# Modulation vectors beside the second branch projection: the sample's half from VectorE to ScalarE and GpSimd

## The chip, the cores and the metric

The kernel runs on one core of a Trainium2 chip. The core has five engines that work side by side, each through its own instructions in order: TensorE (PE in the profile; PEld is its weight load), VectorE (DVE), ScalarE (ACT), GpSimd (POOL) and SyncE (SP), which here only issues DMAs. The metric is the device time of one execution in microseconds (us), lower is better.

## The reference, cut to what matters

One layer of a streaming encoder is computed for two groups of rows at once, a prompt of 512 frames and a sample of 64. The change touches the modulation vectors alone, and it runs while the second branch is projected:

```
mod = silu(c) @ w_ada + b_ada                  # c: one vector for the prompt, one for the sample
sh1, sc1, gt1, sh2, sc2, gt2 = split(mod, 6)   # w_ada is 1024 x 6144
...
mixed = (g_attn * (o_attn @ w_branch_attn) + g_ssm * (y @ w_branch_ssm)) @ w_out
x = x + gt1 * mixed
h2 = rms_normalize(x) * g_norm_ffn * (1.0 + sc2) + sh2
```

## The kernel before, in words

Every matrix product splits its operands into a high and a low part (`wh`, `wl` of the weights, `yh`, `yl` of the rows), and TensorE multiplies high by high, low by high and high by low. The 576 columns of prompt and sample together go through in two halves of 288. For the second branch projection (the loop over `a` in range(8) that makes `ps = fm(f"pbs{a}", ...)`), each output tile a takes 16 row tiles k, so 96 matmuls. Its weights come in two chunks of eight k: a DMA fills `raw`, ScalarE writes `wh`, VectorE writes `wl` as `raw - wh`. Three buffers of each exist, so ScalarE can write the next `wh` once TensorE has left an old one. When a tile a is done, VectorE makes `g` from the PSUM result, adds it to `m`, and `m` is split into `mh` (ScalarE) and `ml` (VectorE) for the output projection.

Beside this, `ada_columns(u, adv)` (L792, called at L1604 to L1606) computes five sets of 512 modulation columns, u = 5 to 9, without TensorE's main work: `w_ada` comes in row blocks of 128 (tile `adr`), and for each row block kt and each group s (0 the prompt, 1 the sample) one VectorE instruction multiplies the block by the group's column of `sil` and adds it to the accumulator `aacc` of that group. After eight blocks `ada_sum` (L809) adds over the partitions: eight matmuls against the constant `pick` (four for each group, `px<-aacc,pick` in the order, sixteen records in the profile), VectorE copies the result (`ra`), TensorE transposes it (`py<-ident,ra`), VectorE adds the bias (`modc`). These results are wanted in the stages behind.

The order is not that of the code. `Plan.add` (L289) records each instruction, `Plan.order` plays a schedule with a table of costs and writes every engine's list in that order, and each engine then follows its list. The plan treats GpSimd instructions that read wide operands, and VectorE instructions with two wide SBUF inputs, as exclusive to each other (`op.port`). A TensorE instruction is placed at least `slack` after its inputs in the plan: 3.0 us for the `pick` matmuls, 0.25 us (`SLACK`) otherwise, the transposition of `ra` included. All instructions go through one line (L544), so the profile tells them apart by their tiles.

Of the kernel before, what the change touches and what calls it, by code (L numbers as in the profile page):

```python
# [5 lines left out]
F32 = mybir.dt.float32  # L6
F32R = mybir.dt.float32r
BF = mybir.dt.bfloat16
AF = mybir.ActivationFunctionType
OP = mybir.AluOpType  # L10
# [3 lines left out]
P = 128  # L14
# [216 lines left out]
def _cols(v):  # L231
    n = 1
    for k in v.shape[1:]:
        n *= k
    return n


def is_psum(v):
    return isinstance(v, View) and v.base.kind == "psum"
# [9 lines left out]
class Plan:  # L249
# [39 lines left out]
    def add(self, eng, fn, args, kw):  # L289
        op = Op()  # L290
        op.eng, op.fn, op.args, op.kw = eng, fn, args, kw
        op.i, op.succ, op.pools, op.bytes, op.mm = len(self.ops), [], set(), 0, False
        op.prio = op.i - self.offset
        outs = [args[0] if args else kw["out"]]
        if kw.get("accum_out") is not None:
            outs.append(kw["accum_out"])
        outs = [o for o in outs if isinstance(o, View)]
        ins = [a for a in list(args[1:]) + [v for k, v in kw.items() if k not in ("out", "accum_out")] if isinstance(a, View)]
        deps = {}
        for v in ins:  # L300
            self._touch(op, v, False, deps)
        for v in outs:
            self._touch(op, v, True, deps)
        for o in self.also:
            deps.setdefault(o.i, "raw")
        op.deps = deps
        op.slack = self.slack if eng == "tensor" else 0.0
        wide = sum(1 for v in ins if not is_psum(v) and _cols(v) > 1)
        op.port = eng == "gpsimd" and wide > 0 and fn != "dma_start" or eng == "vector" and wide > 1
        op.dur, op.dur_dma = self.cost(op, outs, ins)  # L310
        self.ops.append(op)
        return op
# [239 lines left out]
def build(tc, I, O):  # L552
    R = Plan(tc)
    vec, act, pool, pe, sync = R.vec, R.act, R.pool, R.pe, R.sync
# [11 lines left out]
    def px(name, tag="px"):  # L566
        return psum.tile([P, 512], F32, name=name, tag=tag, bufs=2)
# [49 lines left out]
    raws, outs, outs_made = {}, {}, []  # L617
# [107 lines left out]
    sil = adp.tile([P, 8, 32], F32, name="sil")  # L725
# [63 lines left out]

    acc_last = {}  # L790

    def ada_columns(u, pl, nacc=1, bufs=2, nk=2, tags=None, late=False):  # L792

        acc = [pl.tile([P, 512], F32, name=f"aacc{u}{s}", tag=tags[s] if tags else f"aacc{s}", bufs=nacc) for s in range(2)]
        for k0 in range(0, 8, nk):
            raw = pl.tile([P, nk, 512], F32, name=f"wada{u}_{k0}", tag=tags[2 + k0 // nk % 2] if tags else "adr", bufs=bufs)
            (pool if u == 10 else sync).dma_start(raw, w_ada[P * k0:P * (k0 + nk), 512 * u:512 * u + 512].rearrange("(k p) n -> p k n", p=P))
            for j in range(nk):
                kt = k0 + j
                for s in range(2):  # L800
                    if kt == 0:
                        vec.tensor_scalar(acc[s], raw[:, j], sil[:, kt, s:s + 1], None, op0=OP.mult)
                    else:
                        acc_last[u, s] = vec.scalar_tensor_tensor(acc[s], raw[:, j], sil[:, kt, s:s + 1], acc[s], op0=OP.mult, op1=OP.add)
        if late:
            return acc
        ada_sum(u, acc, px(f"padc{u}"))

    def ada_sum(u, acc, p, p2=None):  # L809
        with R.prio(4000):  # L810
            R.slack = 3.0
            with R.after([acc_last[u, s] for s in range(2)]):
                for s in range(2):
                    for g in range(4):
                        pe.matmul(p[32 * g:32 * g + 32, 0:P], pick[:, s], acc[s][:, P * g:P * g + P], start=(s == 0), stop=(s == 1),
                                  tile_position=(0, 32 * g))
            R.slack = SLACK
            ada_out(u, p, p2)
# [26 lines left out]
    for tb in range(5):  # L845
# [5 lines left out]
        for k4 in range(2):  # L851
            p = px(f"pxn{tb}_{k4}")
            for j in range(4):
                kt = 4 * k4 + j
# [53 lines left out]
    with R.prio(-1500):  # L908
        for tb in range(5):
# [9 lines left out]
            for k4 in range(2):  # L919
                o, i = st[:, 4 * k4:4 * k4 + 4, :n], p[:, k4].rearrange("p (k q) -> p k q", k=4)[:, :, :n]  # L920
# [166 lines left out]
    with R.prio(0):  # L1087
        ada_columns(4, adx, 1, 1, 1)
# [88 lines left out]
    for c in range(5):  # L1177
        o, i0 = (p[0][:32, P * c:P * c + P], P) if c < 4 else (p[1][:32, :NS], NS)
# [21 lines left out]
    for b in (4, 1, 2, 3):  # L1200
# [4 lines left out]
        s = ix.tile([P, n], F32, name=f"score{b}")  # L1205
# [106 lines left out]
    for kv in range(NKV):  # L1312
# [21 lines left out]
        for un in units + [None]:  # L1334
            nxt = None
            if un is not None:
                b, qs, k0, n, nk, v0, w = un
# [244 lines left out]
    for s, dst in ((0, O["conv_prompt"]), (1, O["conv_sample"])):  # L1582
        p = px(f"pcvo{s}")
        pe.transpose(p[:96, :P], cvo[:, s].rearrange("p j a -> p (j a)"), ident)
        o = sd.tile([96, P], F32, name=f"cvoT{s}")
# [14 lines left out]
    with R.prio(0):  # L1600
        for u in range(4 + NADX, 4 + NADX + NADA):
            ada_columns(u, gtp, 2)
    adv = R.mkpool("adav", reuse_waits="tile")
    with R.prio(-2000):  # L1604
        for u in range(4 + NADX + NADA, 10):
            ada_columns(u, adv)  # L1606
    yh_p = R.mkpool("yhl", reuse_waits="tile")
    yh = [yh_p.tile([P, T], F32R, name=f"yh{k}") for k in range(16)]
    yl = [yh_p.tile([P, T], F32R, name=f"yl{k}") for k in range(16)]
# [368 lines left out]
    xo, acc = {}, {}  # L1978
# [184 lines left out]
    for o in order:  # L2163
# [27 lines left out]
        else:  # L2191
            s, r, p = o[1:]
# [72 lines left out]
```

## Time and profile before

| | |
|---|---|
| median of 3 runs | 1355.69 us (1355.35 to 1356.16) |
| span of the profiled execution, first to last instruction | 1353.9 us |
| TensorE (PE) busy | 1341.1 us, 99% |
| VectorE (DVE) busy | 1138.9 us, 84% |
| ScalarE (ACT) busy | 756.7 us, 56% |
| GpSimd (POOL) busy | 247.9 us, 18% |
| TensorE's granted clock, mean | 0.999 of full speed |

The page states the span of the profiled execution and no other time for it; the median of the runs lies 1.8 us above that span, which is what the execution takes around its first and last instruction. Busy time is the time in which an engine had an instruction running. Times of rows are counted from the first instruction.

### The profile page before, as it was taken

Reading aid. Unit: us, or ns where it says so; the run is one execution under the profiler, and the core shown is the slowest. Engines: PE = TensorE matmul, PEld = TensorE weight load, DVE = VectorE, ACT = ScalarE, POOL = GpSimd, SP = SyncE. Lnnn points to the kernel's source line nnn. Section 1 sums busy time; section 2 is a strip of 40 time slices with the busy share of each in tenths; the row PEclk is TensorE's granted clock in tenths of the full one; section 3 lists DMA queues with packets and bytes.
Section 4 is the critical chain, followed back from the end, with each engine's and each line's share of the span. In section 5 each row is a group of like instructions: output and inputs, shape, how many; then the busy total and the mean of one; then the engine's idle time right before and its main releaser. Section 6 shows DMA issues by size and latency. Waiting matters only on the chain.

```text
span 1353.9 us, 27909 instructions
## 1 busy us (share of the span) xinstructions
PE 1341.1 (99%) x10677; PEld 1307.3 (97%) x10677; DVE 1138.9 (84%) x2303; ACT 756.7 (56%) x1597; POOL 247.9 (18%) x381
## 2 busy tenths in 40 slices
PE   8999999999999999999999999999999999999998
PEld 6999999999999999999999999999999999999998
DVE  5788999887777788888887688867799999878997
ACT  5445343787777666666565342225576666665453
POOL 2312011230301234545463300002100000000000
PEclk9999999999999999999999999999999999999999
DMA  9762435574754464454445688747533343324352
GB/s 300 228 182 82 112 107 155 126 184 108 170 139 119 139 177 112 116 151 129 133 122 172 216 290 256 232 139 250 153 94 94 99 129 102 94 78 138 98 163 64
DMA packets 268454, 201.35 MB, mean 149 GB/s; under 512 B 25553, under 2 KB 239681, under 8 KB 268321
## 3 DMA queue, kind: packets, MB, share of 16 engines
q1 hardware_dynamic: 263056, 183.40, 46.2%
q0 software_dynamic: 4976, 16.05, 5.9%
q8 instruction: 83, 1.36, 0.4%
q14 instruction: 51, 0.41, 0.1%
q10 hardware_dynamic: 288, 0.13, 0.0%
HBM read 157.75 MB, written 28.96 MB: 138 GB/s over the span
## 4 chain that ended last, share of the span: by engine, by line
PE 93%; DVE 4%; issue 1%; ACT 1%; DMA 0%; POOL 0%; DVEq 0%; POOLq 0%; ACTq 0%
PE mm L544 64%; PE py L544 17%; PE px L544 12%; DVE score L544 1%; DVE m L544 1%; DVE wl L544 0%; DMA B<-in_w_down 0%; DVE tok L544 0%; DVE xs L544 0%; DVE rr L544 0%; ACT wh L544 0%; ACT wl L544 0%; POOL tok L544 0%; DVE xn L544 0%; DVE kst L544 0%
## 5 line engine op out<-in xcount | busy, mean ns | idle before, releaser
L544 ACT ACTIVATE wh<-raw 128x1024 fp32r<-128x1024 f32 (+3 forms) x144 | 140.5, 979 | 170.5 <-PE mm L544 133.0
L544 PE MATMUL mm<-hTl,wh 128*128 128x288 f32 (+1 forms) x1024 | 232.7, 302 | 0.9 <-DVE hTl L544 0.9
L544 PE MATMUL mm<-hTh,wh 128*128 128x288 f32 (+1 forms) x1024 | 231.6, 303 | 0.6 <-ACT wh L544 0.5
L544 PE MATMUL mm<-hTh,wl 128*128 128x288 f32 (+1 forms) x1024 | 230.3, 302 | 0.0
L544 PEld LDWEIGHTS mm<-hTl,wh 128*128 128x128 f32 (+1 forms) x1024 | 166.9, 189 | 3.7 <-DVE hTl L544 1.4
L544 PEld LDWEIGHTS mm<-hTh,wh 128*128 128x128 f32 (+1 forms) x1024 | 166.0, 189 | 4.0 <-ACT hTh L544 1.0
L544 PEld LDWEIGHTS mm<-hTh,wl 128*128 128x128 f32 (+1 forms) x1024 | 165.8, 189 | 1.8 <-issue 0.7
L544 DVE TENSOR_TENSOR wl<-raw,wh 128x1024 fp32r<-128x1024 f32 (+2 forms) x99 | 120.9, 1223 | 25.5 <-ACT wh L544 24.3
L544 POOL DMA_DIRECT2D wl<-raw x24 | 22.1, 919 | 472.2 <-PE px L544 313.8
L544 DVE SCALAR_TENSOR_TENSOR cu<-xc,wc,cu 128x579 f32<-128x579 f32 x96 | 83.8, 873 | 2.0 <-ACT cu L544 1.0
L544 PE MATMUL mm<-wh,hTl 128*128 128x256 f32 x256 | 73.2, 286 | 0.0
L544 PE MATMUL mm<-wl,hTh 128*128 128x256 f32 x256 | 72.5, 284 | 0.0
L544 PE MATMUL mm<-wh,hTh 128*128 128x256 f32 x256 | 72.4, 285 | 0.0
L544 DVE SCALAR_TENSOR_TENSOR aacc<-adr,sil,aacc 128x512 f32<-128x512 f32 x84 | 59.1, 753 | 5.0 <-DMA adr<-in_w_ada 4.7
L544 PE MATMUL mm<-yh,wl 128*128 128x288 f32 x256 | 55.2, 296 | 0.0
L544 PE MATMUL mm<-yh,wh 128*128 128x288 f32 x256 | 55.0, 296 | 0.0
L544 PE MATMUL mm<-yl,wh 128*128 128x288 f32 x256 | 54.9, 296 | 0.0
L544 PE MATMUL mm<-xhS,wh 128*128 128x290 f32 (+1 forms) x248 | 54.8, 296 | 0.0
L544 ACT ACTIVATE P<-lg,mn 128x128 f32<-128x128 f32 (+4 forms) x72 | 41.7, 580 | 23.1 <-DVE mn L544 22.0
L544 PE MATMUL mm<-xhS,wl 128*128 128x290 f32 (+1 forms) x232 | 51.2, 296 | 0.0
L544 ACT ACTIVATE dec<-dec,nacs 128x128 f32<-128x128 f32 x128 | 42.4, 392 | 14.4 <-POOL dec L544 14.4
L544 PEld LDWEIGHTS mm<-wh,hTl 128*128 128x128 f32 x256 | 48.3, 189 | 0.4
(569 smaller groups left out, 4077.9 us busy)
## 6 DMA issues: line engine op xcount, KB each, us to landing
raw<-in_w_in SPq DMA_DIRECT2D x80, 512.0 KB, 4.2
adr<-in_w_ada SPq DMA_DIRECT2D x36, 512.0 KB, 5.5
raw<-in_w_gate_up SPq DMA_DIRECT2D x22, 512.0 KB, 3.8
wl<-raw POOLq DMA_DIRECT2D x21, 512.0 KB, 4.9
rawu<-in_w_gate_up SPq DMA_DIRECT2D x20, 512.0 KB, 3.8
bc<-acs_d SPq DMA_DIRECT2D x32, 256.0 KB, 3.5
raw<-in_w_branch_ssm SPq DMA_DIRECT2D x16, 512.0 KB, 4.8
gate_d<-sg SPq DMA_DIRECT2D x16, 288.0 KB, 2.4
```

The costliest lines, as they stand in the source:

```text
L544: getattr(engines[x.eng], x.fn)(*[real(a) for a in x.args], **{k: real(v) for k, v in x.kw.items()})
```

## The change

`ada_columns` gets an argument, `split_add`, and the five sets call it with one row block per load instead of two, three load buffers instead of two, and `split_add=True`. For the sample (s = 1) ScalarE then multiplies the block by the scale into a tile `prod` of one buffer (the first block straight into the accumulator), and GpSimd adds `prod` to the accumulator. The prompt (s = 0) stays on VectorE as it was. In the plan, GpSimd's adds into `aacc` no longer count as exclusive to VectorE.

```diff
@@ Plan.add
         wide = sum(1 for v in ins if not is_psum(v) and _cols(v) > 1)
-        op.port = eng == "gpsimd" and wide > 0 and fn != "dma_start" or eng == "vector" and wide > 1
+        shared = eng == "gpsimd" and isinstance(outs[0], View) and outs[0].base.name.startswith("aacc")
+        op.port = eng == "gpsimd" and wide > 0 and fn != "dma_start" and not shared or eng == "vector" and wide > 1
@@ ada_columns
-    def ada_columns(u, pl, nacc=1, bufs=2, nk=2, tags=None, late=False):
+    def ada_columns(u, pl, nacc=1, bufs=2, nk=2, tags=None, late=False, split_add=False):
...
                 for s in range(2):
-                    if kt == 0:
+                    if split_add and s:
+                        o = pl.tile([P, 512], F32, name=f"prod{u}_{kt}", tag="prod", bufs=1) if kt else acc[s]
+                        act.activation(o, raw[:, j], AF.Copy, scale=sil[:, kt, s:s + 1])
+                        if kt:
+                            acc_last[u, s] = pool.tensor_tensor(acc[s], acc[s], o, OP.add)
+                    elif kt == 0:
                         vec.tensor_scalar(acc[s], raw[:, j], sil[:, kt, s:s + 1], None, op0=OP.mult)
                     else:
                         acc_last[u, s] = vec.scalar_tensor_tensor(acc[s], raw[:, j], sil[:, kt, s:s + 1], acc[s], op0=OP.mult, op1=OP.add)
@@ the five sets
         for u in range(4 + NADX + NADA, 10):
-            ada_columns(u, adv)
+            ada_columns(u, adv, 1, 3, 1, split_add=True)
```

The lists of all engines are the same before and behind this stage; inside it they differ at these places.

ScalarE while set u = 7 is computed, from one weight split to the fourth behind it (`mh` is the high part of a finished output tile). Before:

```order
L544 ACTIVATE wh_101<-raw_99 128x1024
L544 ACTIVATE wh_102<-raw_100 128x1024
L544 ACTIVATE mh_0_9330<-m_9349 128x2x256
L544 ACTIVATE mh_0_9330<-m_9349 128x2x32
L544 ACTIVATE wh_103<-raw_99 128x1024
L544 ACTIVATE wh_101<-raw_100 128x1024
```

And now (`aacc_0_9039` is the sample's accumulator):

```order
L545 ACTIVATE wh_101<-raw_99 128x1024
L545 ACTIVATE prod_9043<-adr_9042,sil_119 128x512
L545 ACTIVATE aacc_0_9039<-adr_9041,sil_119 128x512
L545 ACTIVATE prod_9043<-adr_9040,sil_119 128x512
L545 ACTIVATE wh_102<-raw_100 128x1024
L545 ACTIVATE prod_9043<-adr_9041,sil_119 128x512
L545 ACTIVATE mh_0_9312<-m_9331 128x2x256
L545 ACTIVATE prod_9043<-adr_9042,sil_119 128x512
L545 ACTIVATE mh_0_9312<-m_9331 128x2x32
L545 ACTIVATE prod_9043<-adr_9040,sil_119 128x512
L545 ACTIVATE wh_103<-raw_99 128x1024
L545 ACTIVATE prod_9043<-adr_9041,sil_119 128x512
```

Up to three products now stand between two weight splits; one more product follows the last row shown, and then the fourth split.

TensorE around set 7's selection (`pick`) and transposition; `yh_0_9045` is row tile k = 0 before, `yh_0_9047` now. Before:

```order
L544 MATMUL mm_115<-yh_0_9045,wh_102 128x288 x2
L544 MATMUL mm_115<-yl_0_9061,wh_102 128x288 x2
L544 MATMUL px_112<-aacc_0_9038,pick_120 32x128 x4
L544 MATMUL px_112<-aacc_0_9039,pick_120 32x128 x4
L544 MATMUL mm_115<-yh_0_9045,wl_105 128x288 x2
L544 MATMUL mm_115<-yh_0_9046,wh_102 128x288 x2
L544 MATMUL mm_115<-yl_0_9062,wh_102 128x288 x2
L544 MATMUL mm_115<-yh_0_9046,wl_105 128x288 x2
L544 MATMUL py_110<-ident_70,ra_122 128x128
```

And now:

```order
L545 MATMUL mm_115<-yl_0_9065,wh_102 128x288 x2
L545 MATMUL mm_115<-yh_0_9049,wl_105 128x288 x2
L545 MATMUL px_112<-aacc_0_9038,pick_120 32x128 x4
L545 MATMUL px_112<-aacc_0_9039,pick_120 32x128 x4
L545 MATMUL mm_115<-yh_0_9050,wh_102 128x288 x2
L545 MATMUL mm_115<-yl_0_9066,wh_102 128x288 x2
L545 MATMUL mm_115<-yh_0_9050,wl_105 128x288 x2
L545 MATMUL mm_115<-yh_0_9051,wh_102 128x288
L545 MATMUL py_110<-ident_70,ra_122 128x128
```

The selection moved from behind the fourth matmul of its tile to behind the eighteenth, and seven matmuls instead of eight lie between it and the transposition. The selections of sets 5, 6, 8 and 9 moved back by 30, 18, 3 and 9 matmuls.

VectorE in front of the copy `ra` of set 7. Before:

```order
L544 SCALAR_TENSOR_TENSOR g_9348<-g_9348,mm_114 128x576
L544 TENSOR_TENSOR m_9350<-m_9350,g_9348 128x576
L544 COPY ra_122<-px_112 128x128
L544 TENSOR_TENSOR wl_104<-raw_100,wh_101 128x1024
L544 TENSOR_TENSOR modc_74<-py_110,badc_75 128x8
```

And now:

```order
L545 SCALAR_TENSOR_TENSOR g_9330<-g_9330,mm_114 128x576
L545 TENSOR_TENSOR m_9332<-m_9332,g_9330 128x576
L545 TENSOR_TENSOR wl_104<-raw_100,wh_101 128x1024
L545 TENSOR_TENSOR ml_0_9321<-m_9332,mh_0_9313 128x2x256
L545 COPY ra_122<-px_112 128x128
```

The weights' low part and the finished tile's low part now stand ahead of the copy.

## Rows read from the trace of the kernel before

**Rows 1.** Page: span; busy time of each engine, share, instructions.
```profile
span 1353.9 us, 27909 instructions
...
PE 1341.1 (99%) x10677; PEld 1307.3 (97%) x10677; DVE 1138.9 (84%) x2303; ACT 756.7 (56%) x1597; POOL 247.9 (18%) x381
```

**Rows 2.** Chain that ended last, 784 to 960: start, us, what.
```profile
784.52 32.52 PE mm L544 x244
...
837.50 0.57 PE px L544 x16
...
856.21 0.57 PE px L544 x16
...
877.04 0.57 PE px L544 x16
...
898.25 46.38 PE mm L544 x348
```

**Rows 3.** Stretches: length, busy us by engine, PEclk, DMA share, GB/s.
```profile
core 0: us, PE busy (x) PEld busy (x) DVE busy (x) ACT busy (x) POOL busy (x), PEclk, DMA share, GB/s
...
790.00:817.00 27.00, 27.00 (x207) 26.83 (x207) 24.63 (x35) 12.05 (x15) 0.00 (x0) 1.00 1.04 349
```

**Rows 4.** VectorE by form, 790 to 897.5: busy us, mean ns; idle before.
```profile
L544 DVE SCALAR_TENSOR_TENSOR aacc<-adr,sil,aacc 128x512 f32<-128x512 f32 x70 | 48.6, 747 | 0.8 <-DMA adr<-in_w_ada 0.6
...
L544 DVE TENSOR_TENSOR wl<-raw,wh 128x1024 fp32r<-128x1024 f32 x17 | 20.7, 1219 | 4.4 <-ACT wh L544 4.4
...
L544 DVE SCALAR_TENSOR_TENSOR g<-g,mm 128x576 f32<-128x576 f32 x10 | 7.5, 751 | 7.7 <-PE mm L544 7.5
...
L544 DVE TENSOR_TENSOR yl<-stage,yh 128x576 fp32r<-128x576 f32 x10 | 7.3, 754 | 0.4 <-ACT yh L544 0.3
...
L544 DVE TENSOR_TENSOR m<-m,g 128x576 f32<-128x576 f32 x7 | 5.3, 756 | 0.2
...
L544 DVE TENSOR_SCALAR aacc<-adr,sil 128x512 f32<-128x512 f32 x10 | 4.6, 481 | 0.0
...
L544 DVE TENSOR_TENSOR ml<-m,mh 128x512 fp32r<-128x512 f32 x6 | 4.1, 683 | 0.0
```

**Rows 5.** ScalarE by form, the same stretch.
```profile
L544 ACT ACTIVATE wh<-raw 128x1024 fp32r<-128x1024 f32 x17 | 18.0, 1059 | 64.5 <-PE mm L544 47.7 <-issue 16.8
...
L544 ACT ACTIVATE mh<-m 128x512 fp32r<-128x512 f32 x7 | 4.4, 634 | 8.2 <-DVE m L544 8.2
```

**Rows 6.** ScalarE by form, whole run: a Copy-sized pass with a per-partition operand.
```profile
L544 ACT ACTIVATE P<-lg,mn 128x512 f32<-128x512 f32 x16 | 11.5, 718 | 4.9 <-DVE mn L544 4.9
```

**Rows 7.** Tiles cs (GpSimd) and cu (VectorE): ns min/median/max.
```profile
L544 POOL TENSOR_TENSOR cs<-bc,bcx x32: 737/1296/1927, 466.6 to 757.3; 128x512 f32<-128x512 f32 x24, 128x256 f32<-128x256 f32 x8
...
L544 DVE SCALAR_TENSOR_TENSOR cu<-xc,wc,cu x96: 804/818/1753, 454.8 to 734.9; 128x579 f32<-128x579 f32 x96
```

**Rows 8.** Timeline 757 to 759, GpSimd, then VectorE: start, us.
```profile
757.32 1.30 POOL L544 TENSOR_TENSOR cs<-bc,bcx 128x512 f32<-128x512 f32 x1 [0.94 <-PE py L544]
...
757.85 0.75 DVE L544 SCALAR_TENSOR_TENSOR g<-g,mm 128x576 f32<-128x576 f32 x1 [0.16 <-PE mm L544]
...
758.52 1.22 DVE L544 TENSOR_TENSOR wl<-raw,wh 128x1024 fp32r<-128x1024 f32 x1
```

**Rows 9.** Timeline 834 to 878, ScalarE, then VectorE; in brackets, idle before.
```profile
835.86 1.06 ACT L544 ACTIVATE wh<-raw 128x1024 fp32r<-128x1024 f32 x1 [2.60 <-issue]
...
855.51 1.06 ACT L544 ACTIVATE wh<-raw 128x1024 fp32r<-128x1024 f32 x1 [5.18 <-PE mm L544]
...
862.73 1.06 ACT L544 ACTIVATE wh<-raw 128x1024 fp32r<-128x1024 f32 x1 [4.65 <-issue]
...
875.53 1.06 ACT L544 ACTIVATE wh<-raw 128x1024 fp32r<-128x1024 f32 x1 [2.08 <-issue]
...
836.95 1.23 DVE L544 TENSOR_TENSOR wl<-raw,wh 128x1024 fp32r<-128x1024 f32 x1 [2.44 <-ACT wh L544]
...
855.72 0.75 DVE L544 SCALAR_TENSOR_TENSOR g<-g,mm 128x576 f32<-128x576 f32 x1 [2.62 <-PE mm L544]
```

**Rows 10.** DMA issues, 790 to 897.5: KB each, median us to landing.
```profile
adr<-in_w_ada SPq DMA_DIRECT2D x19, 512.0 KB, 4.5
```

## The prediction

> **What bounds the kernel now.** I read the page first: TensorE is busy for 1341.1 of the span's 1353.9 us [rows 1]. Busy matmuls overlap, so a busy engine can still be a waiting one; the chain of waits settles that. From 784.52 on it runs through TensorE alone: 244 matmuls in 32.52 us, then the selections and transpositions of the modulation sets, then 348 in 46.38 us [rows 2]. Both stretches give 0.133 us per matmul, the same with VectorE nearly full (24.63 of 27 us) and with the DMA engines saturated (349 GB/s, share 1.04), at the full clock [rows 3]. So in the stage that the change touches TensorE is never late, and an engine that is relieved there shortens nothing. The prediction is therefore about whether the new work makes TensorE wait.
>
> **What goes and what comes.** The change takes 35 multiply-adds of 0.747 us and 5 products of 0.481 us from VectorE [rows 4], 28.5 us. On the path they were worth nothing: TensorE's work covers them.
>
> ScalarE gets 40 products of 512 columns. The trace has none, so I bound one: a plain pass over 512 columns takes 0.634 us [rows 5], one with a per-partition operand 0.718 us [rows 6]. The product has such an operand, so 0.72 us; 40 are 29 us. ScalarE was busy for 12.05 of 27 us in the fullest part of the stage [rows 3], so its load is no problem. Its order is: behind a product that waits for `prod` stand weight splits and tile splits, for which VectorE and then TensorE wait.
>
> GpSimd gets 35 adds of 128x512 with two SBUF inputs. The same shape has a median of 1.296 us here [rows 7] and 1.30 us in a place where nothing disturbs it [rows 8]; 35 are 45 us on an engine that stood idle. The Trainium skill, GPSIMD Engine Reference, section Engine selection, advises against such adds on GpSimd, as about twice as slow as on VectorE; by that rule the sample's half is dearer, and so it is in the rows, but it is dearer off the path.
>
> SyncE issues 40 loads of 256 KB in place of 20 of 512 KB, with three blocks in flight instead of four. A load of double size lands 4.5 us after its issue [rows 10]. Three buffers then allow three blocks in 4.5 + 0.72 + some 0.4 us, 1.9 us a block, less than the adds below need: hidden. In SyncE's list the weight loads now stand between block loads that wait for products, so they come late by what the chain is late, no more. On GpSimd four small copies move ahead of set 10's loads; they wait for sets 6 and 7, which are done by then.
>
> **The new chain.** There is one `prod` buffer, so products and adds alternate: ScalarE 0.72, GpSimd 1.29, and two hand-overs of 0.03 to 0.05 us each (a weight split that starts at 835.86 ends at 836.92, and VectorE starts on it at 836.95 [rows 9]). That is 2.1 us a block, 73 us for 35, in a stage of 107 us. It fits, but the sets have dates: the selection stands at a fixed place in TensorE's list, and an instruction that waits there holds up everything behind.
>
> **The wait that the plan leaves out.** VectorE and GpSimd get in each other's way. `cu`, a VectorE instruction with two SBUF inputs, takes 0.818 us as a rule and up to 1.753 us, and `cs` on GpSimd 1.296 and up to 1.927 [rows 7]; the long ones lie on each other. Where the VectorE instruction reads one input from PSUM, neither is longer: `g` took 0.75 us inside an add, as always [rows 4, 8]. So an add waits for a VectorE instruction under way, and the reverse. What VectorE has left of that kind is 26.1 (prompt) + 2.4 + 20.7 + 7.3 + 5.3 + 4.1 = 66 us [rows 4], with the adds 111 us by busy time. Busy times overlap by some 0.08 us each (`g` to `wl` is 0.67 us, `g` took 0.75 [rows 8]), so with some 115 instructions about 102 of 107 us are really taken. When an add comes, VectorE is mostly in such an instruction. I take 0.35 us for the wait of one add: about half of the commonest instruction (0.67 us from start to start). Its bounds are nothing and 1.14 us, a `wl` just begun.
>
> **Set by set.** A selection's new date is its old one [rows 2] and 0.133 us for each matmul that it moved back. For set 7: 856.21 + 14 x 0.133 = 858.1. Its chain starts with the selection of set 6, at 837.50 + 18 x 0.133 = 839.9 and 0.57 long, since the accumulator must be free: first product done at 841.2, then 7 adds, 6 products and 13 hand-overs, 9.0 + 4.3 + 0.7 = 14.0 us: 855.2 without waits, 857.7 with 7 of 0.35. It is in time by 0.4 us. Set 8 has only five adds behind the weight split of 862.73 [rows 9], which ends at 863.8: 5 x (2.1 + 0.35) = 12.3, ready at 876.1, wanted at 877.04 + 0.4 = 877.4. Sets 5, 6 and 9 have 0.7, 1.1 and 1.3 us to spare in the same way (five, six and five adds in a row).
>
> The transpositions are tighter. Set 7's stands 0.57 + 7 x 0.133 = 1.5 us behind its selection, at 859.6. VectorE can begin `g` at 855.72 [rows 9], but two of the prompt's instructions end only at 856.3, the last add holds `m` until 857.4, and `m`, `wl`, `ml` and the copy take 0.67 + 1.14 + 0.60 + 0.28: 860.1. TensorE waits 0.5 us. For set 8 the weight split of 875.53 [rows 9] stands behind a product that needs set 8's last add (876.3), so it ends at 878.05; `wl`, one product and the copy follow until 879.9, and the transposition stands at 878.9 + 0.5: another 0.45 us. Sets 5, 6 and 9 just fit. Sum: **+1.0 us**, as nothing behind the stage gives it back. The weight splits, late by up to 3 us behind products, cost nothing: the one that starts at 855.51, when TensorE leaves a buffer, is wanted when it leaves the next, at 862.73 [rows 9]; after 1.06 us for itself and 1.22 for `wl` [rows 4, 5] that is 4.9 us of room.
>
> Against the profiled execution this is 1353.9 + 1.0 = 1354.9 us of span; the runs lie 1.8 us above that span, so 1355.69 + 1.0 = **1356.7 us**.
>
> **The rivals.** *The waits fall between.* If GpSimd mostly finds VectorE waiting for TensorE, the wait of an add is near nothing and so is every lateness: 1355.7. For it: VectorE stood idle 7.5 us before `g` [rows 4], and now has less of its own. Against it: the 102 of 107 us.
>
> *The two engines block each other in full (slower).* With VectorE's next instruction always queued, an add waits for a whole one, 0.67 us in place of 0.35. Then set 7 loses 7 x 0.32 = 2.2 us and is 1.8 late; set 6 is 0.8 late, set 5 0.9, sets 8 and 9 0.3 each: 4.1 us, with the 1.0 of the transpositions 5.1: 1360.8. It decides from a wait of about 0.5 us per add. The Trainium skill, SBUF — State Buffer, section SBUF: two separate sides, calls this pair of ports an exclusive lock that the first comer keeps for the whole instruction. By that rule VectorE loses up to 45 us and gains 28.5, and this rival is the likelier; the durations in rows 7 agree with a lock, and how often the two meet in this stage no row shows.
>
> *Nothing is late and something is gained (faster).* TensorE would have to run faster than 0.133 us per matmul or skip a wait; the chain shows none in 160 us. I see no more than a chance arrangement behind the stage, where four residual steps now stand ahead of set 10's products: at most 3 us, 1352.7.
>
> **How the numbers follow.** About 0.2% (2.7 us) is what a measurement of this kernel can tell from no change. The forecast (small waits, up to 2.7 us) gets 0.45, no waits 0.31, the full blocking 0.21, the gain 0.03. Forecast and no waits both read as the same: 0.76. The range reaches from a microsecond under the median, 1354.6, to 1360.5, which takes in the lower half of the blocking case; some 0.13 is left out.
>
> **What would show it.** In the changed profile: TensorE's chain from 784 to 953 with waits of about half a microsecond at `py<-ident,ra` of sets 7 and 8, and none at `px<-aacc,pick`; 40 products of 0.72 us; 35 adds with a median near 1.6 us, the wait included; VectorE's busy time down by far less than 28.5 us. Wrong: waits of over a microsecond at the selections (the blocking), weight splits that come later than 5 us (ScalarE's order), or a TensorE that starts matmuls closer than 0.133 us.

## The result and the profile after

The changed kernel takes 1364.67 us (median of 4 runs, 1362.33 to 1366.26) against 1355.52 of the kernel before: a ratio of 1.0064, 95% interval 1.005 to 1.0079. It is slower by 0.5 to 0.8%, where 1356.7 us had been forecast and the range ended at 1360.5. The profiled execution is the fastest of the four, 1362.33 us with a span of 1360.6; the span has grown by 6.7 us. The page of the changed kernel, its span and its busy times:

```profile
span 1360.6 us, 28033 instructions
...
PE 1340.6 (99%) x10677; PEld 1305.7 (96%) x10677; DVE 1143.9 (84%) x2263; ACT 783.7 (58%) x1637; POOL 300.9 (22%) x416
```

Beside [rows 1], ScalarE has 27.0 us more and GpSimd 53.0 us, as the new products and adds make it. VectorE lost 28.5 us of work, and yet its busy time rose by 5.0: some 33 us of its records are time in which it was held up. TensorE's busy time fell by 0.5 us in a span longer by 6.7, so it stood still for about that much more. The view of waits for 786 to 906 says for whom (engine and tile, what was waited for, us in total, times, longest):

```profile
ACT prod L545 <- POOL aacc L545: 32.1, 23, 2.5
ACT prod L545 <- DMA adr<-in_w_ada: 12.6, 6, 3.8
...
ACT wh L545 <- PE mm L545: 9.2, 6, 3.6
PEld py L545 <- DVE ra L545: 7.2, 4, 2.7
...
PE py L545 <- DVE ra L545: 6.1, 3, 2.5
...
DVE wl L545 <- ACT wh L545: 3.1, 3, 1.7
...
PEld px L545 <- POOL aacc L545: 0.2, 1, 0.2
```

TensorE (PE, and PEld for its weights) waited at four transpositions, `py<-ident,ra`, for the copy `ra` by VectorE, and at the selections, `px<-aacc,pick`, for at most 0.2 us. From start to start these four steps are 1.67 (set 5), 0.43 (set 6), 2.60 (set 7) and 2.75 us (set 8); with 0.133 us for an ordinary matmul taken off each, 6.9 us is lost, and the span grew by 6.7. So the whole loss of this execution stands at four places. The median lies 2.3 us above it, and what the other three executions lost beyond this one is in no profile. ScalarE, whose `wh` waited only for TensorE to leave a buffer [rows 5], now mostly waits for the adds.

VectorE by form, 790 to 897.5 (busy us, mean ns; idle before), to be read beside [rows 4]:

```profile
L545 DVE SCALAR_TENSOR_TENSOR aacc<-adr,sil,aacc 128x512 f32<-128x512 f32 x34 | 39.4, 1160 | 7.4 <-DMA adr<-in_w_ada 7.0
L545 DVE TENSOR_TENSOR wl<-raw,wh 128x1024 fp32r<-128x1024 f32 x15 | 20.2, 1346 | 3.7 <-ACT wh L545 3.1 <-DMA g<-gate_d 0.4
L545 DVE TENSOR_TENSOR m<-m,g 128x576 f32<-128x576 f32 x6 | 9.2, 1532 | 0.1
L545 DVE TENSOR_TENSOR yl<-stage,yh 128x576 fp32r<-128x576 f32 x10 | 7.2, 755 | 1.6 <-ACT yh L545 1.5
L545 DVE SCALAR_TENSOR_TENSOR g<-g,mm 128x576 f32<-128x576 f32 x9 | 6.7, 744 | 0.0
...
L545 DVE TENSOR_SCALAR aacc<-adr,sil 128x512 f32<-128x512 f32 x5 | 4.3, 866 | 0.0
```

The prompt's multiply-add takes 1.16 us where it took 0.75, `m` 1.53 where it took 0.76, the first product of a set 0.87 where it took 0.48. `g`, with one input in PSUM, kept its 0.74, inside adds too. `yl` kept its 0.76 although it has two inputs in SBUF; of its ten instructions in this stretch only one met an add (in e13 below, the two that began inside an add took 1.32 and 1.51 us). On GpSimd, 790 to 910, the adds:

```profile
L545 POOL TENSOR_TENSOR aacc<-aacc,prod 128x512 f32<-128x512 f32 x35 | 53.8, 1537 | 68.1 <-ACT prod L545 56.3 <-ACT aacc L545 11.8
```

Their minimum is 1.28 us, and 14 of the 35 lie within 0.05 us of the 1.30 of an undisturbed one [rows 8]; the median is 1.45, and the mean of 1.54 holds 0.25 us of waiting per add. VectorE pays more for a meeting than GpSimd: 33 us over 35 adds are 0.95 us per add. The Trainium skill, SBUF — State Buffer, section SBUF: two separate sides, has the two engines share one pair of ports under an exclusive lock; the spared `g` and the stretched rest agree with that.

How a copy comes late shows in the timeline of the changed kernel (start, us, engine, operation; in brackets idle time before and what ended it). First set 7, then set 8:

```profile
856.40 1.77 DVE L545 SCALAR_TENSOR_TENSOR aacc<-adr,sil,aacc 128x512 f32<-128x512 f32 x1
...
858.24 0.33 SPq L545 DMA_DIRECT2D adr<-in_w_ada  x1
...
862.25 0.72 ACT L545 ACTIVATE prod<-adr,sil 128x512 f32<-128x512 f32 x1 [2.91 <-DMA adr<-in_w_ada]
862.88 0.61 ACT L545 ACTIVATE mh<-m 128x512 fp32r<-128x512 f32 x1
...
863.52 0.69 DVE L545 TENSOR_TENSOR ml<-m,mh 128x512 fp32r<-128x512 f32 x1 [1.66 <-ACT mh L545]
864.13 0.28 DVE L545 COPY ra<-px 128x128 f32<-128x128 f32 x1
...
864.47 0.33 PE L545 MATMUL py<-ident,ra 128*128 128x128 f32 x1 [2.31 <-DVE ra L545]
...
881.53 0.72 ACT L545 ACTIVATE prod<-adr,sil 128x512 f32<-128x512 f32 x1 [1.49 <-POOL aacc L545]
882.15 1.04 ACT L545 ACTIVATE wh<-raw 128x1024 fp32r<-128x1024 f32 x1
...
883.89 1.69 POOL L545 TENSOR_TENSOR aacc<-aacc,prod 128x512 f32<-128x512 f32 x1 [2.40 <-ACT aacc L545]
...
883.23 1.22 DVE L545 TENSOR_TENSOR wl<-raw,wh 128x1024 fp32r<-128x1024 f32 x1 [1.66 <-ACT wh L545]
884.37 1.49 DVE L545 TENSOR_SCALAR aacc<-adr,sil 128x512 f32<-128x512 f32 x1
885.78 0.28 DVE L545 COPY ra<-px 128x128 f32<-128x128 f32 x1
...
886.11 0.33 PE L545 MATMUL py<-ident,ra 128*128 128x128 f32 x1 [2.45 <-DVE ra L545]
```

For set 7 the selection had ended by about 861, so the copy could have run then. But ahead of it in VectorE's list stands `ml`, which needs ScalarE's `mh`; and ahead of that in ScalarE's list stands a product of the next set, whose block came late. Its load was issued at 858.24, when VectorE had left the buffer: the multiply-add that began at 856.40 took 1.77 us beside an add, in place of 0.75. The block landed at 862.17, and the product started at 862.25. For set 8 the product waits for an add instead, `wh` behind it and `wl` behind that come late, and then the first product of set 9 on VectorE meets an add and takes 1.49 us in place of 0.48. In both cases the lateness passes through the lists of ScalarE and VectorE before it reaches TensorE.

### The profile page after: what moved, and what is told of

The parts are those of the page before. It is cut to its first block, busy times and chain, and to the rows that moved or that the text cites. A ratio compares the mean times of both kernels' runs of the same rounds, so it can differ in the third digit from the quotient of the medians.

```text
span 1360.6 us, 28033 instructions
## 1 busy us (share of the span) xinstructions
PE 1340.6 (99%) x10677; PEld 1305.7 (96%) x10677; DVE 1143.9 (84%) x2263; ACT 783.7 (58%) x1637; POOL 300.9 (22%) x416
## 4 chain that ended last, share of the span: by engine, by line
PE 85%; DVE 5%; DMA 4%; ACT 2%; POOL 2%; issue 2%; SPq 0%; DVEq 0%; ACTq 0%; POOLq 0%
PE mm L545 57%; PE py L545 16%; PE px L545 12%; DMA adr<-in_w_ada 2%; POOL aacc L545 1%; DVE score L545 1%; DVE m L545 1%; DVE wl L545 1%; DMA stage<-y_d 1%; ACT prod L545 1%; DMA raw<-in_w_in 1%; ACT wh L545 1%; DMA raw<-in_w_branch_ssm 0%; DVE tok L545 0%; DVE xs L545 0%
## 5 line engine op out<-in xcount | busy, mean ns | idle before, releaser
L545 POOL TENSOR_TENSOR aacc<-aacc,prod 128x512 f32<-128x512 f32 x35 | 53.8, 1537 | 68.1 <-ACT prod L545 56.3
L545 DVE SCALAR_TENSOR_TENSOR aacc<-adr,sil,aacc 128x512 f32<-128x512 f32 x49 | 51.9, 1069 | 10.7 <-DMA adr<-in_w_ada 10.3
L545 ACT ACTIVATE prod<-adr,sil 128x512 f32<-128x512 f32 x35 | 25.3, 723 | 44.7 <-POOL aacc L545 32.1
```

Source lines behind the costliest of these rows:

```text
L545: getattr(engines[x.eng], x.fn)(*[real(a) for a in x.args], **{k: real(v) for k, v in x.kw.items()})
```

## The experiments

All times are medians; a ratio is against the kernel before, run beside it (1356.29 to 1356.35 us). The first question was whether the four places are the loss, or only where a shortage of time happens to show.

**e1: more distance at the transposition.** The plan reckons with 0.25 us between a copy's end and its transposition, and 3.0 us ahead of a selection. Here both are 3.0 for sets 5 to 9.

```diff
+        R.slack = 3.0 if 5 <= u <= 9 else SLACK
         pe.transpose(p2[:, 0:P], ra, ident)
+        R.slack = SLACK
```

> Theory A (the place is too tight): TensorE's only new gaps are in front of the four transpositions of sets 5 to 8, 1.4, 0.2, 2.3 and 2.5 us beyond a matmul's step, because each stands 0.25 us behind its copy in the plan and the copy comes up to 2.75 us late. With 3.0 us of distance in the plan instead, all four are covered: 1356 us (1355.3 to 1357), no idle time of TensorE over 0.3 us ahead of the transpositions. Theory B (VectorE and ScalarE are short of time in the whole stage): the lost time comes back in front of matmuls that need a weight split or a selection, as TensorE no longer stands still 6.9 us: 1360 to 1364 us. A half-way case, 1357 to 1359, would mean that one or two of the copies are later than 3.0 us once TensorE doesn't wait for them.

Measured: 1361.52 us, ratio 1.0043 (1.003 to 1.0056). The number is theory B's. In the view of waits of this run the waits have moved one step up:

```profile
PEld px L545 <- POOL aacc L545: 3.4, 4, 1.2
...
PE px L545 <- POOL aacc L545: 2.4, 4, 0.9
...
PEld py L545 <- DVE ra L545: 0.5, 1, 0.5
```

With hardly a wait at a transposition the selections come earlier, and now the sample's sums on GpSimd are late for them. Whether that is a shortage or a second tight place this run does not tell.

**e11: more distance at both.** As e1, and 6.0 us instead of 3.0 ahead of the selections of sets 5 to 9.

```diff
-            R.slack = 3.0
+            R.slack = 6.0 if 5 <= u <= 9 else 3.0
```

> The changed kernel with more distance in the plan ahead of TensorE's work on sets 5 to 9: the transposition 3.0 us (0.25 before) and the selection 6.0 us (3.0 before). With 3.0 us at the transposition alone, TensorE stood 0.4 to 1.1 us ahead of the selection's second half at five sets, 4 us in all. Theory A (only places are too tight; TensorE has other work for the time): 1355.5 to 1357.5 us, no idle time over 0.4 us at either. Theory B (the vector engines are short of time): the waits move on to weight splits or later sets, 1359 to 1362 us.

Measured: 1357.05 us, ratio 1.0004 (0.9995 to 1.0014): not to be told from the kernel before. TensorE has no gap left in the stage. Nothing was made faster here: adds, loads and VectorE's stretched instructions (aacc at 1.10 us) are those of the changed kernel. Theory B falls; what was lost was lost to places in TensorE's list, at the selections and at the transpositions.

The second question was what makes the copies late: the loads, the meeting of VectorE and GpSimd, or the length of GpSimd's step.

**e2: the loads alone**, in the kernel before.

```diff
-            ada_columns(u, adv)
+            ada_columns(u, adv, 1, 3, 1)
```

> The kernel before with one edit: its blocks are loaded one at a time into three buffers, as in the changed kernel; the arithmetic stays on VectorE. Theory A (instructions of VectorE are stretched beside the adds): loads alone make no copy late, 1355.5 to 1356.3 us. Theory C (the loads make the products and sums late: one block took 7.4 us from its issue to landing, another 3.75): the transpositions wait here too, 1358 to 1361 us.

Measured: 1358.07 us, ratio 1.0017 (1.0008 to 1.0026). One transposition waits, that of set 5, 2.2 us by the view of waits; the others do not. It is the low edge of theory C: the loads by themselves cost about 2 us, at set 5, where VectorE stood idle 3.8 us for a block by the timeline of this run. That block landed 7.5 us after its issue, and the one at the same place in the changed kernel 7.4 us after. The prediction had called the loads hidden.

**e3: narrow adds.** The same order (the plan is told the add's old cost), but an add of one column.

```diff
-acc_last[u, s] = pool.tensor_tensor(acc[s], acc[s], o, OP.add)
+acc_last[u, s] = pool.tensor_tensor(acc[s][:, 0:1], acc[s][:, 0:1], o[:, 0:1], OP.add)
...
+        if shared:
+            op.dur = (512 * 2.1 + 150) / 1e3
```

> The changed kernel in the same order, its GpSimd adds one column wide instead of 512, so that the sample's sums of sets 5 to 9 are not computed beyond the first product but for that column. Theory A (the adds stretch VectorE's instructions with two inputs from SBUF): the aacc instruction falls from 1.18 to 0.75 us, m from 1.42 to 0.76, ts from 0.87 to 0.48, the copies are in time but for at most one, and the time is 1356 to 1357.5 us. Theory C (loads and ScalarE's products make them late): the waits at sets 5 and 7, behind products that waited for a load, stay, 1359 to 1362 us.

Measured: 1355.85 us, ratio 0.9997 (0.9988 to 1.0006), and no wait over 0.2 us. By form, VectorE's instructions are back (aacc 0.749, m 0.756 us); the add takes 0.48 us:

```profile
L547 POOL TENSOR_TENSOR aacc<-aacc,prod 128x1 f32<-128x1 f32 x35 | 16.7, 477 | 94.6 <-ACT prod L547 71.4 <-ACT aacc L547 22.2 <-DVE aacc L547 1.1
```

With the loads and products of the change in place, and with the order of every list as in the changed kernel, nothing is lost, not even at set 5; presumably a VectorE with half the work makes up for late blocks, as one with all of it (e2) does not. So the adds are needed for the loss. But a narrow add is both shorter and without traffic.

**e10 and e12: as long as the adds, without their traffic.** A power on 7 columns, then one on 5, stand for the add; the plan's cost and the order are those of e3.

```diff
-acc_last[u, s] = pool.tensor_tensor(acc[s], acc[s], o, OP.add)
+acc_last[u, s] = pool.tensor_tensor(acc[s][:, 0:7], ones[:, 0:7], o[:, 0:7], OP.pow)
```

> The changed kernel in the same order, each GpSimd add of 512 columns replaced by a power on 7 columns, which by GpSimd's powers elsewhere in the program (5 columns 1.17 us, 10 columns 1.97 us) keeps it busy about 1.5 us, as long as the adds took (1.54), but reads and writes next to nothing of SBUF; the sample's sums of sets 5 to 9 are left out beyond the first product. Theory P (the add stretches VectorE's instructions with two inputs from SBUF, since the two share a port): aacc back at 0.75 us, m at 0.76, and 1355.5 to 1357 us. Theory D (the add's length holds up ScalarE through the one product buffer, and so the splits and sums): the waits stay, 1360 to 1364 us. If VectorE is stretched here as well, it is GpSimd's being busy, not its traffic, that holds VectorE up.

> As the run with powers on 7 columns (1.61 us each in place, 1361.05 us in all, no VectorE instruction stretched), but on 5 columns, which take 1.17 us elsewhere in the program; the plan reckons with 1.23 us for the add. The sample's sums of sets 5 to 9 are again left out beyond the first product. Theory D (GpSimd's step, longer than the plan reckons, holds up ScalarE's next product and the splits behind it): now the step fits the plan, 1355.5 to 1357 us. If the chain product, add, product over one buffer is too slow at any length over 1 us, 1359 to 1361 us.

Measured: 1361.05 us (ratio 1.0032, 1.002 to 1.0045) with 7 columns, 1356.92 (1.0005, 0.9996 to 1.0015) with 5. By form, of the run with 7 columns, VectorE's prompt sum and GpSimd:

```profile
L547 DVE SCALAR_TENSOR_TENSOR aacc<-adr,sil,aacc 128x512 f32<-128x512 f32 x35 | 26.2, 748 | 11.6 <-DMA adr<-in_w_ada 11.3
...
L547 POOL TENSOR_TENSOR aacc<-ones,prod 128x7 f32<-128x7 f32 x35 | 56.5, 1614 | 63.6 <-ACT prod L547 52.1 <-ACT aacc L547 11.6
```

No VectorE instruction is stretched, and still about half of the loss is there (a ratio of 1.0032 against 1.0064). So it is the adds' traffic that stretches VectorE, not GpSimd's being busy. An exclusive lock kept for the whole instruction, as in the prediction's second rival, would have had these powers hold VectorE up; with next to nothing read or written they did not. Theory P alone is out: GpSimd's step by its length already makes things late. The 5-column power took 1.29 us on average, and one wait of 0.8 us was left:

```profile
L547 POOL TENSOR_TENSOR aacc<-ones,prod 128x5 f32<-128x5 f32 x35 | 45.1, 1288 | 68.8 <-ACT prod L547 54.2 <-ACT aacc L547 14.6
```

In one and the same order a step of 0.48 us loses nothing, one of 1.29 loses 0.6 us, which is not clear of noise, and one of 1.61 loses 4.7 us. But 1.29 us is the length of an undisturbed add (1.28). So the add's own length costs little or nothing; what costs is the meeting with VectorE, which makes the add longer (1.54 us) and VectorE's instructions too. The timeline of the 7-column run shows how a long step makes things late, at set 8; the load is a piece of the chain of waits:

```profile
873.05 0.72 ACT L547 ACTIVATE prod<-adr,sil 128x512 f32<-128x512 f32 x1 [0.65 <-POOL aacc L547]
...
873.80 5.01 DMA adr<-in_w_ada
...
878.90 0.72 ACT L547 ACTIVATE prod<-adr,sil 128x512 f32<-128x512 f32 x1 [2.66 <-DMA adr<-in_w_ada]
879.52 1.04 ACT L547 ACTIVATE wh<-raw 128x1024 fp32r<-128x1024 f32 x1
...
880.60 1.22 DVE L547 TENSOR_TENSOR wl<-raw,wh 128x1024 fp32r<-128x1024 f32 x1 [4.10 <-ACT wh L547]
...
882.13 0.28 DVE L547 COPY ra<-px 128x128 f32<-128x128 f32 x1
...
882.47 0.33 PE L547 MATMUL py<-ident,ra 128*128 128x128 f32 x1 [2.72 <-DVE ra L547]
```

The product at 873.05 waited for the step before; its end, at 873.78, frees a block's buffer. The next load is issued at 873.80 and lands 5.01 us later, and the product that needs it waits 2.66 us, with the split behind it. A long step delays the product, the product the load, the load a later product.

**e13: two blocks per load again**, with the products and adds of the change.

```diff
-            ada_columns(u, adv, 1, 3, 1, split_add=True)
+            ada_columns(u, adv, split_add=True)
...
-        ra = adp.tile([P, P], F32, name=f"ra{u}", tag="ra", bufs=2)
+        ra = adp.tile([P, P], F32, name=f"ra{u}", tag="ra", bufs=1)
```

> The changed kernel with the loads of the kernel before: two blocks in one transfer, two buffers of two (and one buffer for the copy ahead of a transposition instead of two, to make room). One-block loads alone cost 1.8 us in the kernel before, at set 5. If the loads are a part by itself, 1361 to 1363.5 us. If they carry most of the loss (a product that waits for a block is what makes the split behind it late), 1356 to 1360 us. If they add nothing beside the adds, 1364 to 1366 us.

Measured: 1359.83 us, ratio 1.0026 (1.0016 to 1.0035). Over half of the loss goes with the old loads, far more than the 2 us that the new ones cost alone. So the parts do not simply add up. That they feed each other along the loop just shown is argued, not shown: the plan wrote another order for this run (set 7's selection stands some 20 matmuls further forward than in the changed kernel), and what that order gives is not told apart from what the loads give. What is left are waits of 1.5 us at one transposition and up to 1.0 us at two selections.

**e5: two product buffers**, so that ScalarE need not wait for each add (and one buffer for `ra`, as in e13).

```diff
-tag="prod", bufs=1)
+tag="prod", bufs=2)
```

> The changed kernel with two product buffers instead of one (and one buffer for the copy ahead of a transposition instead of two, to make room). Theory D: ScalarE no longer waits for the add of the product before last, its 32 us of waits on adds shrink to under half, the weight's and the row-tile's high halves come in time, 1356 to 1359 us. Theory P: VectorE's instructions stay stretched (aacc near 1.15 us), the copies stay late, 1360 to 1364 us.

Measured: 1364.84 us, ratio 1.0068 (1.0055 to 1.0081), no gain. The view of waits of this run:

```profile
ACT prod L545 <- DMA adr<-in_w_ada: 31.8, 15, 5.0
...
ACT prod L545 <- POOL aacc L545: 4.6, 6, 1.0
...
PE px L545 <- DVE aacc L545: 3.7, 2, 2.8
```

The wait for the adds fell from 32.1 to 4.6 us as theory D said, and the wait for blocks rose from 12.6 to 31.8. The plan put the work in another order here, and TensorE's longest waits are now selections that want the prompt's sums, on a VectorE whose aacc takes 1.13 us. Theory D's time did not come, and theory P's stretching and late work did, with a time 0.8 us above its range. So freeing ScalarE from the adds is not enough where VectorE stays stretched; how much of this run's loss is the other order, it does not tell.

**e6: the adds on VectorE.**

```diff
-acc_last[u, s] = pool.tensor_tensor(acc[s], acc[s], o, OP.add)
+acc_last[u, s] = vec.tensor_tensor(acc[s], acc[s], o, OP.add)
```

> The changed kernel with the adds on VectorE instead of GpSimd; ScalarE's products, the loads and the buffers stay. VectorE has 35 adds of 0.65 to 0.75 us in place of the 35 instructions that the change took from it, so its work is as before. Theory P (meeting of GpSimd and VectorE): no instruction is stretched, what is left is what the one-block loads alone cost (1.8 us), 1356.5 to 1359 us. Theory S (ScalarE's products themselves, 0.72 us each ahead of the high halves, are what is late): 1360 us or more.

Measured: 1357.57 us, ratio 1.0013 (1.0004 to 1.0022). Nothing is stretched (aacc 0.745, the new add 0.686 us), and one wait is left, 2.7 us at set 5, the place at which the loads alone cost 2.2. ScalarE's products cost nothing beside that which this run could tell.

**e4 and e9: the plan is told of the meeting.** In e4 the exemption of these adds is taken back, so that no VectorE instruction with two SBUF inputs is planned beside one; e9 adds the 3.0 us of e1 to that.

```diff
-        op.port = eng == "gpsimd" and wide > 0 and fn != "dma_start" and not shared or eng == "vector" and wide > 1
+        op.port = eng == "gpsimd" and wide > 0 and fn != "dma_start" or eng == "vector" and wide > 1
```

> The changed kernel with the adds counted by the plan like GpSimd's other work (no VectorE instruction with two inputs from SBUF is planned beside one); the operations are the same. Theory A: the plan now places copies and transpositions later, about where they come, and the waits shrink to under 2 us in all, 1356 to 1357.5 us. Theory B (short of time): VectorE's work no longer fits, waits move to the weight splits, 1360 us or more. Theory C: the adds' place in the plan doesn't matter, loads still come late, 1359 to 1363 us.

> Both cures together: the adds counted by the plan like GpSimd's other work (alone 1357.4 us, with one wait left, 2.2 us ahead of the transposition of set 5) and 3.0 us of distance ahead of the transpositions of sets 5 to 9. If places are all that is wrong: no idle time of TensorE in the stage over 0.4 us, 1355.5 to 1356.7 us, as the kernel before and not below it, since TensorE has no idle time there to give back. If VectorE and GpSimd are short of time even so: 1357.5 us or more.

Measured: e4 1357.43 us (1.0011, 1.0002 to 1.002) with one wait left, 2.1 us at set 5 (in the profiled execution, 1359.06 us); e9 1356.02 us, ratio 0.9994 (0.9986 to 1.0003). The stage in e9, by stretches (length, busy us of PE, PEld, DVE, ACT and POOL, PEclk, DMA share, GB/s), and two of VectorE's forms:

```profile
820.00:840.00 20.00, 20.00 (x163) 19.64 (x162) 19.83 (x21) 9.86 (x14) 10.87 (x8) 1.00 0.75 232
840.00:860.00 20.00, 20.00 (x162) 19.64 (x162) 16.19 (x20) 8.96 (x13) 10.00 (x7) 1.00 0.72 212
860.00:880.00 20.00, 20.00 (x163) 19.63 (x162) 18.16 (x19) 9.37 (x14) 10.33 (x7) 1.00 0.73 222
```

```profile
L545 DVE SCALAR_TENSOR_TENSOR aacc<-adr,sil,aacc 128x512 f32<-128x512 f32 x31 | 35.7, 1152 | 3.8 <-DMA adr<-in_w_ada 3.3
...
L545 DVE TENSOR_TENSOR m<-m,g 128x576 f32<-128x576 f32 x6 | 8.8, 1462 | 0.1
```

VectorE is as stretched as in the changed kernel and nearly full, and TensorE does not stand still once. This is the change without its loss, and it is level with the kernel before: where TensorE has no idle time to begin with, there is none to give back. No run was faster than the kernel before by more than the interval.

## Why the prediction was wrong

- **What bounds the kernel, and no gain from the relief:** right. TensorE sets the end; e3, e9 and e11, all without waits, are level with the kernel before and not below it.
- **Product 0.72, add 1.29, hand-overs:** right. Measured 0.72 us, and 1.28 us for the least disturbed add. An add's wait was put at 0.35 us and was 0.25 on average; the blocking rival needed 0.5.
- **The selections in time:** they were, but by luck. The sums were ready later than reckoned, at 860.1 in place of 857.7 for set 7 and at 881.5 in place of 876.1 for set 8, by the timeline of the changed kernel. They came in time only because the transpositions of the sets before had by then held TensorE up: set 7's selection stood at 860.4, not at 858.1. Without that the selections are up to 1.2 us late (e1), so the margins of 0.4 to 1.3 us were not there.
- **The transpositions, +1.0 us:** this is the term that failed. The place was right and the size was not: 0.5 and 0.45 us were forecast at sets 7 and 8, and 2.5 and 2.6 came; sets 5 and 6, which "just fit", lost 1.5 and 0.3. That is 6.9 us in place of 1.0. The sum for set 7 let `m`, `wl`, `ml` and the copy follow each other at once; `ml` in fact waited 1.66 us for `mh`, which stands behind a product. Two steps lie behind the wrong size, the next two.
- **"Hidden" for the loads:** wrong. 1.9 us a block was set against the 2.1 us of the adds, as if both ran side by side. But a block is issued only when the last reader has left its buffer, a late product (e10) or a stretched multiply-add (set 7), and the product that needs it waits for it to land, 4.0 us from issue to product in the case of set 7. At set 5 a block took 7.4 us to land where 4.5 had been taken. With the old loads, and the order that the plan wrote for them, over half of the loss is gone (e13).
- **What an add does to VectorE:** counted only where an add met `m` of set 7. In fact VectorE's larger forms with SBUF inputs were longer by 0.1 to 0.8 us on average, all but `yl`; it is some 33 us in all against 28.5 us of relief. Of the 2.2 us that set 8 lost beyond its forecast, 1.0 is the first product of the next set, which takes 1.49 us behind an add.
- **Weight splits late by up to 3 us at no cost:** right for TensorE's use of the weights, which it never waited for. But the same split stands ahead of the copy in VectorE's list, and there its lateness counted.
- **The rivals:** the full blocking had the nearer time, 1360.8, by another way (late selections, 0.67 us a meeting), and neither came. A case was missing in which the loop of product, add and load runs behind as a whole, and the transpositions of four sets pay for it.

That the meeting of the adds with VectorE is the cause is shown by e3, e12 and the changed kernel, which share one order. What stays open is how the loss divides between the stretching of VectorE and the length that the meeting gives to GpSimd's step. Without stretching, e10 lost 4.7 us (2.7 to 6.1) of the 9.1, but its step of 1.61 us is longer than the adds' 1.54; a straight line between e12 and e10 gives 3.8 us for 1.54, an estimate. No run had the stretching with a short step.

## What to carry to other kernels

In a list of instructions whose order is fixed ahead, ask of every instruction of the bound engine how late the one it needs may come, and follow that one's queue back through every engine: the tightest distance decided here (0.25 us in the plan), not how busy the engines are. Where the bound engine has no idle time, moving work to an idle engine gained nothing in any run here, and could cost; if it is done all the same, tell the planner of what the two engines do to each other (that alone brought the loss from 9 us to 1) and give all the tight places room (that alone, to 0.7, which is not clear of noise; at the transpositions only, to 5).

## What was not expected of the hardware

After some of the waits TensorE's granted clock fell for a few microseconds. In the 7-column run TensorE stood still from about 879.7 to 882.47, and then, by stretches of 2 us (PEclk is the last but two):

```profile
880.00:882.00 2.00, 0.00 (x0) 0.00 (x0) 1.40 (x2) 1.18 (x2) 0.75 (x1) 1.00 0.19 67
882.00:884.00 2.00, 1.53 (x11) 1.53 (x12) 1.90 (x5) 0.72 (x1) 1.17 (x2) 0.96 0.45 136
884.00:886.00 2.00, 2.00 (x10) 2.00 (x10) 0.00 (x0) 0.00 (x0) 1.47 (x1) 0.50 1.04 350
886.00:888.00 2.00, 2.00 (x13) 2.00 (x13) 0.75 (x1) 0.20 (x1) 0.00 (x0) 0.69 0.46 171
888.00:890.00 2.00, 2.00 (x18) 2.00 (x17) 1.86 (x2) 1.47 (x2) 0.45 (x1) 1.00 0.00 0
```

0.50 is 1.2 of 2.4 GHz; what is missing from full speed in these rows, 0.08 + 1.0 + 0.62, is 1.7 us on top of a wait of 2.7. Taken as PE's own waits, the same fall stands behind the 2.0 us of e2 and the 2.8 us of e5, and none stands behind the 2.3 and 2.5 us of the changed kernel's profile, the 2.5 us of e6 or the 1.9 us of e4. So waits of like length came with a fall and without one; with one they cost 1.7 us more, and executions of one kernel can then differ by that much. In e10's profiled execution, too, part of the loss is this fall and not waiting. That the changed kernel's other three executions (spans of 1362.5 to 1363.3 us) contain such falls is likely by their mean granted clocks (0.997 and 0.998, against 0.999), and was not shown.
